# Delta rule's inverse: sums of two levels and the last sum move from identity matmuls to VectorE

## Chip, cores and metric

The kernel runs on one core of one Trainium2 chip. The metric is device time in microseconds (us). Before the change three runs gave 920.37, 923.16 and 924.47 us; the median is 923.16.

## The reference, cut to what matters

One layer of a generator: a modulated input, one input projection, two groups of heads on its columns, one output projection, a layer norm. The first group is a diagonal state-space scan (S5). The second is a gated delta rule with four heads and two directions, over 256 context and 1024 latent tokens in chunks of 64. For each chunk the reference solves a unit lower triangular system and then scans the chunks:

```python
a_mat = jnp.where(strict, bc[..., :, None] * kk * decay, 0.0)
sol = lax.linalg.triangular_solve(a_mat + eye, rhs, left_side=True, lower=True, unit_diagonal=True)
u0, w = sol[..., :Dv], sol[..., Dv:]
# then, for each chunk in turn:
u = ui0 - w_i @ s
o = g_i * (q_i @ s) + qk_i @ u
s = gl_i * s + k_i.T @ u
```

The kernel takes chunks of 128 tokens instead and forms the inverse of the triangular matrix itself. The change lies in that inverse.

## The kernel before, in words

Up to about 540 us the kernel computes the modulation, the projections, the S5 group and the convolutions of the second group. Then comes the delta rule, until about 845 us, and last the end of the last head's scan with the output projection and the norm.

In the delta rule each of the four heads has ten chunks of 128 tokens. One call of `tbatch` (line 1173) makes the inverses of two chunks in both directions, four 128x128 matrices u = 0 to 3 side by side in tiles of 128x512; five calls make a head, 20 the kernel. A call builds the decay (`mg`, `pd`, `dec`, lines 1185 to 1211), the products of keys and of keys with queries (`pk`, 1212), the matrix `tt` and its fp16 copy `t16`, and the start of the inverse in `xz`, an fp16 tile of 128 x 4 x 2 x 128 which holds the inverse's blocks (xs) and their transposes (zs).

The inverse then grows by doubling blocks, in the loop of line 1269 over levels l = 1 to 6. A level is four steps in a row: eight small matmuls into the bank `pp` (line 1274); a masked copy of them into the fp16 tile `pad` (VectorE at line 1282, at level 6 ScalarE at 1277); sixteen small matmuls into the bank `px` (line 1298); and `xz` plus `px` back into `xz`. This last step has two forms. At the levels in `ACTL`, which are 1 and 3, line 1290 first puts the old `xz` into the bank by a product with the identity, the sixteen matmuls add to it, and ScalarE copies the bank to `xz` (line 1309). At levels 2, 4 and 5 there is no identity product and VectorE adds bank and `xz` (line 1311). Level 6 is copied by ScalarE (line 1304).

After the loop one step of iteration refines the inverse: the residual `r16` (lines 1315 to 1325), the bank `pzz` = residual times zs (1328), a scaled copy `dl` (1330), residual times `dl` added to the same bank (1332), and then 1024 times zs added to it by two products with `i1k`, which is 1024 times the identity (line 1337; the tile is made at line 111). `finish` copies the bank to the fp32 tile `zf` with the factor 1/1024 on ScalarE (line 1360).

All banks of one call share one PSUM bank of its own (`bank`, tag t0 to t3): four calls can be under way, and within a call a bank must be emptied before the next step writes it. `scan_head` (line 1370) then runs ten steps for both directions: `s1` (matmul, line 1386), `rr` (VectorE, 1390), `s2` with `zf` (1395), `uu` (ScalarE, 1399), `s3` (1402), `st` (VectorE, 1409), and for latent chunks the output (1416, 1417). Between all this `fill` queues pieces of a part of the output projection (`poa`, `part_out`) behind given matmuls.

The engines run in parallel, each in a fixed order of its own. That order is worked out when the kernel is built, by the framework's planner from its own estimate of each instruction (the kernel is built with `schedule_with_timeline_sim=True`, line 1673): batches, the scan of the head before and the output projection are mixed by it. What is changed in one instruction can therefore change the order elsewhere.

Of the kernel before, what the change touches and what calls it, by code (L numbers as in the profile page):

```python
# [11 lines left out]
F16 = mybir.dt.float16  # L12
BF16 = mybir.dt.bfloat16
I32 = mybir.dt.int32
AF = mybir.ActivationFunctionType
ALU = mybir.AluOpType
# [3 lines left out]
P = 128  # L20
# [21 lines left out]
def tile_hybrid_block(  # L42
# [30 lines left out]
    V, S, G, T, Q = nc.vector, nc.scalar, nc.gpsimd, nc.tensor, nc.sync  # L73

    per = ctx.enter_context(tc.tile_pool(name="per", bufs=1))
# [13 lines left out]
    def bc(ap, shape):  # L89
        return ap.to_broadcast(shape)  # L90

    ident = per.tile([P, P], F32, name="ident")
# [3 lines left out]
        out=sel,  # L96
# [10 lines left out]
    V.tensor_copy(idbf, ident)  # L107
    nid2k = per.tile([P, P], F16, name="nid2k")
    V.tensor_scalar(nid2k, ident, -2048.0, None, op0=ALU.mult)
    i1k = per.tile([P, P], F16, name="i1k")  # L110
    V.tensor_scalar(i1k, ident, 1024.0, None, op0=ALU.mult)
    tri = per.tile([P, 2, P], F32, name="tri")
    trir = per.tile([P, 2, P], F32R, name="trir")
    negm = per.tile([P, 2, P], BF16, name="negm")
# [42 lines left out]
    for t, i, base, cm, step in ((tri, 0, 0, -1, 1), (tri, 1, 0, 1, -1), (trs, 1, -1, -1, 1), (trs, 0, -1, 1, -1)):  # L157
        G.affine_select(
            out=t[:, i, :], in_=t[:, i, :], pattern=[[step, P]], compare_op=ALU.is_ge, fill=0.0,
# [913 lines left out]
    for l in range(1, 7):  # L1073
# [4 lines left out]
        for d in range(2):  # L1078
            V.tensor_scalar(
                lvm[:, l - 1, d].rearrange("p c f -> p (c f)"), eq, half[:, d, l:l + 1], -1.0 / 2048,  # L1080
                op0=ALU.mult, op1=ALU.mult,
# [49 lines left out]
    for st in ORD.split():  # L1131
        name, _, hold = st.partition(">")
# [17 lines left out]
                glu_stage()  # L1150


    ACTL = (1, 3)
    L6, MASKP, NOID, XZP = True, True, True, True
    QTB = 2
    PTB, QGB, WB = 6, 5, 6
# [16 lines left out]
    def tbatch(hd, hs, cp, si):  # L1173
# [5 lines left out]
        def bank(n):  # L1179
            return psT.tile([P, 512], F32, tag=f"t{si}", name=n + nm, bufs=1)  # L1180

        def tl(shape, dt, tag, n):
            return gt_.tile(shape, dt, tag=tag, name=n + nm, bufs=TB[tag])
# [17 lines left out]
        for d in range(2):  # L1201
            for i in range(2):
                u = d * 2 + i
# [3 lines left out]
            if MASKP:  # L1207
                G.affine_select(
                    out=dec[:, d], in_=dec[:, d], pattern=[[0, 2], [1 - 2 * d, P]], compare_op=ALU.is_ge, fill=0.0,
# [3 lines left out]
        for i in range(2):  # L1213
            T.matmul(pk[:, i * P:(i + 1) * P], kT[:, c0 + i, :], kT[:, c0 + i, :], start=True, stop=True)
            if lat:
                T.matmul(
                    pk[:, (2 + i) * P:(3 + i) * P], kT[:, c0 + i, :], qT[:, (c0 + i) * P:(c0 + i + 1) * P],
                    start=True, stop=True,
# [13 lines left out]
        xz = tl([P, 4, 2, P], F16, "xz", "xz")  # L1232
# [4 lines left out]
        if XZP:  # L1237
            G.affine_select(
                out=xz[:, 3::-2], in_=mb.rearrange("p (d c) f -> p d c f", d=2), pattern=[[0, 2], [0, 2], [1, P]],
                compare_op=ALU.not_equal, fill=1.0, base=0, channel_multiplier=-1,  # L1240
            )
        else:
# [5 lines left out]
            out=thi, in_=t16, pattern=[[0, 4], [1, P]], compare_op=ALU.not_equal, fill=2048.0,  # L1248
# [5 lines left out]
            out=tlo, in_=tlo, pattern=[[0, 4], [1, P]], compare_op=ALU.not_equal, fill=0.0,  # L1254
# [6 lines left out]
        def scat(t, b, gs, n):  # L1261
            base = t
            return bass.AP(tensor=base.tensor, offset=base.offset, ap=[list(base.ap[0]), [gs + b, 2], [2 * b, n], [1, b]])
# [5 lines left out]
        for l in range(1, 7):  # L1269
# [16 lines left out]
            px = bank(f"px{l}_")  # L1286
            on_act = l in ACTL
            xo = scat(xz[:, 0, 0], b, 512, 256 // b)
# [30 lines left out]
        r16 = tl([P, 4, P], F16, "r16", "r16")  # L1319
        S.activation(r16.rearrange("p u f -> p (u f)"), prr, AF.Copy, scale=-0.5)  # L1320
        if NOID:
            G.affine_select(
                out=r16, in_=r16, pattern=[[0, 4], [1, P]], compare_op=ALU.not_equal, fill=0.0,
                base=0, channel_multiplier=-1,
            )
        pzz = bank("pzz")
        for u in range(4):
            T.matmul(pzz[:, u * P:(u + 1) * P], r16[:, u, :], zs[u], start=(u == 0), stop=(u == 3))
        dl = tl([P, 4, P], F16, "dl", "dl")
        S.activation(dl.rearrange("p u f -> p (u f)"), pzz, AF.Copy, scale=1.0 / 1024.0)  # L1330
        for u in range(4):
            T.matmul(
                pzz[:, u * P:(u + 1) * P], r16[:, u, :], dl[:, u, :], start=False, stop=False,
                skip_group_check=True,
            )
        for d in range(2):
            T.matmul(
                pzz[:, d * 256:(d + 1) * 256], i1k, xz[:, 3 - 2 * d].rearrange("p c f -> p (c f)"),
                start=False, stop=(d == 1), skip_group_check=True,
            )  # L1340
        def gqs():
            qg = gs.tile([P, 2, 2, P], F32, tag="qg", name="qg" + nm, bufs=QGB)
            for i in range(2):
                Q.dma_start(
                    qg[:, :, i, :], d_gr[c0 + i:c0 + i + 1, hd].to_broadcast([P, 2, P]),
                )
            qv = qT[:, c0 * P:(c0 + 2) * P].rearrange("p (o c f) -> p o c f", o=1, c=2)
            G.tensor_tensor(qg, qg, bc(qv, [P, 2, 2, P]), op=ALU.mult)
            hs["qg"][cp] = qg
# [5 lines left out]
        def finish():  # L1355
            if lat and cp not in hs["qg"]:
                gqs()
            kt = hs["kt"]
            zf = gs.tile([P, 2, 2, P], F32, tag="zf", name="zf" + nm, bufs=WB)
            S.activation(zf.rearrange("p d c f -> p (d c f)"), pzz, AF.Copy, scale=1.0 / 1024.0)  # L1360
            ks = gs.tile([P, 2, 2, P], F32, tag="ks", name="ks" + nm, bufs=WB)
            G.tensor_tensor(
                ks, bc(kt[:, None, c0:c0 + 2, :], [P, 2, 2, P]), bc(gx[:, :, 1, c0:c0 + 2, hd, None], [P, 2, 2, P]),
                op=ALU.mult,
            )
            hs["zf"][cp], hs["ks"][cp] = zf, ks
# [226 lines left out]
    for si in range(NPAD):  # L1593
        mkpads(si)
    fin = [tbatch(0, hs[0], CPS[n], n) for n in range(2)]
    wos.append(rp.tile([P, 2, 4, D], F32R, tag="wo", name="wo_a"))
    load_wo(0)
# [13 lines left out]
    for hd in range(HEADS):  # L1611
        if hd:
            hs[hd] = head_prep(hd)
            head_prep2(hd, hs[hd])
        for cp in CPS:
            if nb > 1:
                tbatch(hd, hs[hd], cp, nb % NS)()
            nb += 1
            if nb == 4 * NS:
                for _ in filler:  # L1620
                    pass
                wos.append(rp.tile([P, 2, 4, D], F32R, tag="wo", name="wo_b"))
                load_wo(1)
        if hd < HEADS - 1:
            scan_head(hd, hs[hd])
            head_out(hd, hs[hd])
# [51 lines left out]
```

## Time and profile before

| | |
|---|---|
| median of three runs | 923.16 us |
| profiled execution | 919.21 us, span 917.5 us |
| TensorE matmul busy | 814.1 us (89%) |
| VectorE busy | 672.5 us (73%) |
| ScalarE busy | 415.2 us (45%) |
| GpSimd busy | 392.1 us (43%) |

In the rows below PE is TensorE's matmuls, PEld its weight loads, DVE is VectorE, ACT is ScalarE, POOL is GpSimd; L1290 is line 1290. Matmuls overlap one another, so the durations of neighbours don't add up to the time that they take. The profiled execution is one run; its span is what the profile covers, and 1.7 us lie around it.

### The profile page before, as it was taken

The numbers are of one execution on the slowest core, as the hardware profiler recorded it, in microseconds if no ns is written. First come the engines' busy times: TensorE is split into PE (matmuls) and PEld (weight loads), VectorE is DVE, ScalarE is ACT, GpSimd is POOL, SyncE is SP. The second block draws the span as 40 slices with busy tenths as digits, with TensorE's granted clock in tenths as the row PEclk, the third lists the DMA queues.
The fourth block names the chain that finished last, engine by engine and source line by source line (L and its number), as shares of the span: only waits on it lengthen the run. The fifth ranks groups of instructions, "written<-read, shape, count | busy, mean of one in ns | idle before, by whom it ended". The sixth has DMA issues, their size and how long they took to land. (4 is left out here: it accounts for less than half of the span.)

```text
span 917.5 us, 17187 instructions
## 1 busy us (share of the span) xinstructions
PE 814.1 (89%) x6553; PEld 674.8 (74%) x6553; DVE 672.5 (73%) x1318; ACT 415.2 (45%) x944; POOL 392.1 (43%) x463
## 2 busy tenths in 40 slices
PE   4988999997898999996899896899989889789994
PEld 2656897785786788874688674687988778678882
DVE  7988986996776778799573388567685585676686
ACT  1321435324434444431544376465763473556353
POOL 3215240007897940100311078874874485441163
PEclk9999999999798999998799897799999999999998
DMA  9981557412304232243454476421135234315332
GB/s 245 302 158 42 196 157 232 146 36 79 132 24 142 106 104 84 94 159 93 122 148 134 148 269 213 145 75 59 48 109 161 82 115 156 128 41 182 126 126 93
DMA packets 120125, 119.49 MB, mean 130 GB/s; under 512 B 21406, under 2 KB 95702, under 8 KB 119914
## 3 DMA queue, kind: packets, MB, share of 16 engines
q1 hardware_dynamic: 101946, 85.42, 32.7%
q10 hardware_dynamic: 18096, 32.97, 9.5%
q8 instruction: 51, 0.84, 0.4%
q14 instruction: 32, 0.26, 0.1%
HBM read 81.33 MB, written 37.04 MB: 129 GB/s over the span
## 5 line engine op out<-in xcount | busy, mean ns | idle before, releaser
L713 POOL TENSOR_TENSOR rta<-ebuf,ar 128x64 f32<-128x64 f32 x38 | 24.8, 653 | 85.3 <-DVE ebuf L688 82.6
L847 POOL COPY hq<-ebuf 64x1024 f32<-64x1024 f32 x8 | 16.4, 2068 | 93.9 <-DVE ebuf L688 58.5
L1187 POOL TENSOR_TENSOR mg<-tri,ghi 128x512 fp32r<-128x512 f32 x20 | 23.2, 1162 | 70.7 <-PE pd L1195 35.4
L1282 DVE TENSOR_TENSOR pad<-pp,lvm 128x256 f16<-128x256 f32 x100 | 40.5, 416 | 16.3 <-PE pp L1274 15.6
L141 PE MATMUL pjz<-h_hi,wtz 128*128 128x512 f32 x128 | 52.0, 406 | 0.1
L142 PE MATMUL pjz<-h_lo,wtz 128*128 128x512 f32 x128 | 52.0, 407 | 0.0
L143 PE MATMUL pjz<-h_hi,wtz 128*128 128x512 f32 x128 | 51.3, 401 | 0.0
L1298 PEld LDWEIGHTS <-xz 128*128 128x128 f16 x480 | 37.6, 101 | 18.5 <-issue 12.5
L1298 PE MATMUL px<-pad,xz 128*128 128x64 f16 x480 | 42.8, 198 | 7.0 <-DVE pad L1282 6.5
L1311 DVE TENSOR_TENSOR xz<-px,xz 128x512 f16<-128x512 f32 x60 | 40.6, 684 | 10.8 <-PE px L1298 8.8
L759 DVE SCALAR_TENSOR_TENSOR cak<-crk,cwt,cak 128x945 f32<-128x945 f32 (+2 forms) x32 | 39.3, 1229 | 7.3 <-ACT cak L749 6.9
L759 DVE SCALAR_TENSOR_TENSOR caq<-crq,cwt,caq 128x945 f32<-128x945 f32 (+2 forms) x32 | 39.2, 1224 | 7.2 <-ACT caq L749 5.3
L1298 PE MATMUL px<-xz,pad 128*128 128x64 f16 x480 | 42.8, 198 | 0.0
L759 DVE SCALAR_TENSOR_TENSOR cav<-crv,cwt,cav 128x945 f32<-128x945 f32 (+2 forms) x32 | 39.4, 1231 | 4.1 <-ACT cav L749 3.8
L1274 PE MATMUL pp<-xz,t 128*128 128x64 f16 x480 | 33.1, 197 | 7.1 <-DVE xz L1311 3.3
L803 POOL TENSOR_TENSOR kss<-kss,mhalf 128x4 f32<-128x4 f32 (+1 forms) x12 | 15.6, 1309 | 55.5 <-DVE kss L802 55.5
L1399 ACT ACTIVATE uu<-s 128x128 f32<-128x128 f32 x80 | 21.0, 275 | 38.7 <-PE s L1395 38.5
L1390 DVE SCALAR_TENSOR_TENSOR rr<-s,ngx,vt 128x128 f32<-128x128 f32 x72 | 24.5, 344 | 17.0 <-PE s L1386 16.4
L1274 PEld LDWEIGHTS <-t 128*128 128x128 f16 x480 | 27.5, 101 | 12.4 <-issue 10.4
L141 PE MATMUL u<-wu,h_lo 128*128 128x512 f32 x64 | 29.3, 458 | 5.5 <-DVE h_lo L562 5.5
L822 ACT ACTIVATE csz<-pjz 128x512 f32<-128x512 f32 x16 | 9.2, 597 | 54.9 <-PE pjz L143 43.0
L1395 PE MATMUL s<-rr,zf 128*128 128x128 f32 x144 | 31.4, 303 | 2.3 <-DVE rr L1390 1.8
(514 smaller groups left out, 3029.1 us busy)
## 6 DMA issues: line engine op xcount, KB each, us to landing
wad<-in_w_ada_dram SPq DMA_DIRECT2D x16, 512.0 KB, 6.3
xk<-in_x_dram SPq DMA_DIRECT2D x8, 512.0 KB, 6.5
d_e<-et ACTq DMA_DIRECT2D x8, 512.0 KB, 2.8
etl<-d_e SPq DMA_DIRECT2D x8, 512.0 KB, 4.3
wg<-in_w_ada_dram SPq DMA_DIRECT2D x8, 512.0 KB, 5.7
wrz<-in_w_in_dram SPq DMA_DIRECT2D x8, 512.0 KB, 3.9
d_z<-csz ACTq DMA_DIRECT2D x8, 512.0 KB, 2.9
xr<-in_x_dram SPq DMA_DIRECT2D x8, 512.0 KB, 5.4
```

The source lines that it names most:

```text
L141: T.matmul(ps, ll, rh, start=first, stop=False)
L142: T.matmul(ps, lh, rl, start=False, stop=False)
L143: return T.matmul(ps, lh, rh, start=False, stop=last)
L713: G.tensor_tensor(ta, prev, ar, op=ALU.mult)
L759: clast[typ, hd] = V.scalar_tensor_tensor(out=o, in0=rv[:, y0 + dy:y1 + dy, x0 + dx:x1 + dx], scalar=cwt[:, t, (dy + 1) * 3 + dx + 1:(dy + ...
L1187: G.tensor_tensor(mg[:, i], bc(tri[:, 0:2, None, :], [P, 2, 2, P]), bc(gsrc[:, :, c0:c0 + 2, hd, None], [P, 2, 2, P]), op=ALU.mult,)
L1274: T.matmul(pp[:, u * 64:(u + 1) * 64], t16[:, u, :], cols(xs[u], b, u // 2), start=True, stop=True)
L1282: V.tensor_tensor(scat(pad[:, 0, :], b, 256, 128 // b), pp[:, :256].rearrange("p (d n b) -> p d n b", d=2, b=b), lvm[:, l - 1].rearrange(" ...
L1298: ins = T.matmul(o, lt, rt, start=not on_act, stop=not on_act or w == 3 and i == 1)
L1311: V.tensor_tensor(xo, pxv, xo, op=ALU.add)
L1390: V.scalar_tensor_tensor(out=rn, in0=p1_[:, :P], scalar=ngx[:, d, ch, hd:hd + 1], in1=rr, op0=ALU.mult, op1=ALU.add,)
L1395: ins = T.matmul(p2_[:, :P], hs["zf"][cp][:, d, i, :], rr, start=True, stop=True)
```

## The change

`ACTL` becomes empty, so that levels 1 and 3 are done as 2, 4 and 5 are: no identity product, and VectorE adds bank and `xz` (line 1311) where ScalarE copied (line 1309). The two products of line 1337 go, with the tile `i1k`; in their place `finish` makes `zf` on VectorE as bank/1024 plus the zs half of `xz`, where ScalarE copied the scaled bank.

```diff
-    i1k = per.tile([P, P], F16, name="i1k")
-    V.tensor_scalar(i1k, ident, 1024.0, None, op0=ALU.mult)
...
-    ACTL = (1, 3)
+    ACTL = ()
...
             T.matmul(
-                pzz[:, u * P:(u + 1) * P], r16[:, u, :], dl[:, u, :], start=False, stop=False,
+                pzz[:, u * P:(u + 1) * P], r16[:, u, :], dl[:, u, :], start=False, stop=(u == 3),
                 skip_group_check=True,
             )
-        for d in range(2):
-            T.matmul(
-                pzz[:, d * 256:(d + 1) * 256], i1k, xz[:, 3 - 2 * d].rearrange("p c f -> p (c f)"),
-                start=False, stop=(d == 1), skip_group_check=True,
-            )
...
-            S.activation(zf.rearrange("p d c f -> p (d c f)"), pzz, AF.Copy, scale=1.0 / 1024.0)
+            V.scalar_tensor_tensor(
+                out=zf, in0=pzz.rearrange("p (d c f) -> p d c f", d=2, c=2), scalar=1.0 / 1024.0, in1=xz[:, 3::-2],
+                op0=ALU.mult, op1=ALU.add,
+            )
```

## Rows read from the trace of the kernel before

**Rows 1.** The page's first table: busy us (share of the span), instructions.
```profile
PE 814.1 (89%) x6553; PEld 674.8 (74%) x6553; DVE 672.5 (73%) x1318; ACT 415.2 (45%) x944; POOL 392.1 (43%) x463
```

**Rows 2.** Busy time by stretch: start:end, length, busy us (instructions), clock, DMA, GB/s.
```profile
580.00:845.00 265.00, 242.46 (x2801) 213.36 (x2799) 176.30 (x414) 151.96 (x435) 152.29 (x184) 0.97 0.32 104
...
545.00:845.00 300.00, 266.05 (x2993) 232.22 (x2991) 206.66 (x455) 169.37 (x468) 184.16 (x214) 0.94 0.36 116
```

**Rows 3.** The same view, 605 to 625 and 685 to 705: their sum.
```profile
sum 40.00, PE 39.90 PEld 35.81 DVE 23.47 ACT 21.69 POOL 26.11; mean PE 19.95 PEld 17.90 DVE 11.74 ACT 10.85 POOL 13.06
```

**Rows 4.** The same view, four other stretches: the first, and the sum of all.
```profile
567.00:577.00 10.00, 4.95 (x58) 3.81 (x59) 9.99 (x16) 4.00 (x8) 10.00 (x11) 0.67 0.91 297
...
sum 40.00, PE 28.20 PEld 23.84 DVE 39.23 ACT 20.27 POOL 30.82; mean PE 7.05 PEld 5.96 DVE 9.81 ACT 5.07 POOL 7.71
```

**Rows 5.** Groups, 545 to 845: busy us, mean ns of one, idle before, releasers.
```profile
L1311 DVE TENSOR_TENSOR xz<-px,xz 128x512 f16<-128x512 f32 x60 | 40.6, 684 | 10.8 <-PE px L1298 8.8 <-ACT pad L1277 1.0 <-ACT uu L1399 0.8
...
L1309 ACT ACTIVATE xz<-px 128x512 f16<-128x512 f32 x40 | 23.6, 593 | 14.0 <-PE px L1298 8.8 <-DVE ml L877 3.5 <-DVE rr L1390 1.2
...
L1290 PE MATMUL px<-xz,id 128*128 128x512 f16 x40 | 16.3, 408 | 1.5 <-DVE pad L1282 1.4
...
L1360 ACT ACTIVATE zf<-pzz 128x512 f32<-128x512 f32 x20 | 11.9, 594 | 8.2 <-PE pzz L1337 8.2
...
L1525 DVE SCALAR_TENSOR_TENSOR y<-xr,poa 128x512 f32<-128x512 f32 x16 | 11.0, 688 | 26.4 <-PE poa L143 17.9 <-DMA xr<-in_x_dram 7.4 <-PE px L1298 1.0
...
L1337 PE MATMUL pzz<-xz,i1k 128*128 128x256 f16 x40 | 7.9, 280 | 0.0
```

**Rows 6.** TensorE's instructions in order of time: start us, us, what.
```profile
592.32 0.38 PE L1290 MATMUL px<-xz,id 128*128 128x512 f16 x1
592.53 0.22 PE L1298 MATMUL px<-pad,xz 128*128 128x64 f16 x2
...
592.99 0.38 PE L1337 MATMUL pzz<-xz,i1k 128*128 128x256 f16 x2
593.21 0.22 PE L1298 MATMUL px<-pad,xz 128*128 128x64 f16 x2
```

**Rows 7.** Busy time by stretch, with the granted clock behind POOL's.
```profile
575.00:585.00 10.00, 7.63 (x94) 6.29 (x94) 6.14 (x12) 4.06 (x9) 10.00 (x11) 0.53 0.85 272
```

**Rows 8.** Chain of waits: shares of 580 to 845, then pieces (start us, us).
```profile
by line: PE px L1298 6.7%; DMA xr<-in_x_dram 6.3%; PE poa L141 5.4%; DMA qg<-d_gr 5.2%; issue 5.2%; PE poa L143 4.7%; PE poa L142 4.7%; PE s L1395 4.3%; PE s L1386 3.7%; PE s L1402 3.5%; PE pp L1274 3.1%; PE s L1416 2.7%; PE pd L1195 2.5%; 
...
582.08 0.43 PE px L1290
...
821.87 0.23 PE px L1290
...
822.55 0.22 PE pzz L1337 x2
...
825.77 0.60 ACT zf L1360
```

**Rows 9.** VectorE's instructions in order of time.
```profile
567.62 0.68 DVE L1224 SCALAR_TENSOR_TENSOR tt<-pkk,dec 128x512 f32<-128x512 f32 x1
568.21 0.68 DVE L1230 TENSOR_TENSOR pt<-pkk,dec 128x512 f32<-128x512 f32 x1
```

**Rows 10.** Busy time by stretch of line 1309 alone, then of line 1360 alone.
```profile
567.00:577.00 10.00, 1.18 (x3) 0.67 0.91 297
...
751.00:757.00 6.00, 1.20 (x2) 1.00 0.06 22
```

**Rows 11.** TensorE's waits, 545 to 845: us in total, times, longest us.
```profile
PE px L1298 <- DVE pad L1282: 6.5, 9, 1.8
...
PE pp L1274 <- DVE xz L1311: 3.3, 6, 0.8
...
PE pp L1274 <- ACT xz L1309: 1.9, 2, 1.1
```

## The prediction, made before the changed kernel was seen

> **What bounds the kernel now.** I read the page's first table, then the busy time by stage, the groups of instructions of the stage that the change touches, TensorE's waits, the chain of waits, and last the single instructions around a few of the removed matmuls. By the page TensorE is the busiest engine (89% of the span), VectorE second (73%) [rows 1]. The changed instructions, one of the start apart, lie between 545 and 845 us. The main part of that stage, 580 to 845, has TensorE busy for 242.5 of 265 us, VectorE 176.3, ScalarE 152.0, GpSimd 152.3 [rows 2]. So TensorE is the first bound there, with gaps of some 22 us. The bound is not the same all along: in two stretches of 20 us TensorE is busy for 39.9 of 40 us [rows 3], but in four others, 567 to 577, 669 to 676, 751 to 757 and 795 to 812, VectorE is, for 39.2 of 40 us [rows 4]. The change takes from TensorE and gives to VectorE, so both kinds of stretch count.
>
> **What goes: TensorE.** Line 1290 (the identity product that opens the bank of levels 1 and 3) runs 40 times, line 1337 (the last sum) 40 times in 20 pairs. The table gives 408 and 280 ns for one [rows 5], but matmuls overlap, so the price is the step from one start to the next: line 1290 starts at 592.32 and the next matmul at 592.53, which is 0.21 us; a pair of line 1337 starts at 592.99 and the next matmul at 593.21, 0.22 us [rows 6]. That is at TensorE's full clock. About five of the 40 start before 585, where the granted clock is 0.53 of full in ten us, thus mostly at the lower of its two levels [rows 7]; they cost twice as much. TensorE issues 40 x 0.21 + 5 x 0.21 + 20 x 0.22 = 13.9 us less. That is the upper bound. The lower bound is nothing: where TensorE would wait anyway, the time was free. Between them the chain of waits decides. Line 1290 stands on it with 20 pieces of 0.21 to 0.43 us, 5.4 us in all, and line 1337 with 15 pairs, nearly all 0.22 us, 3.4 us in all (a long and a typical piece stand) [rows 8]. I take 5.4 + 3.4 = 8.8 us; the other 20 and 5 are off the chain. The identity product cannot hide in the wait for the masked pad: all levels of a batch use one bank, and that is free for line 1290 only when line 1282 on VectorE has read it, the very instruction that the other matmuls of the level wait for. Line 111, a small VectorE operation of the start, I count as nothing: it runs half a millisecond before the stage.
>
> **What goes: ScalarE.** 40 copies of line 1309 at 593 ns and 20 of line 1360 at 594 ns, 35.5 us of its 169.4 between 545 and 845 [rows 2, 5]. ScalarE is not the bound, so this frees nothing by itself. Seven of the copies are on the chain, 3.8 us in all, such as 0.60 us of zf at 825.77 [rows 8].
>
> **What comes: VectorE.** 40 sums more of line 1311's kind, which is there 60 times at 684 ns, and 20 scaled sums for zf. The zf form (bank and fp16 in, fp32 out, 128x512) is not in the trace; nearest are line 1525, the same operation with an fp32 operand at 688 ns, and line 1311 with an fp16 one at 684 [rows 5]. I take 686; the ends are 594 (if it cost what ScalarE's copy costs) and 780 (as far above), which over 20 is 1.9 us either way. On the path a sum is thus 0.09 us longer than the copy: 7 x 0.09 = +0.6 us. In a full queue the step counts: line 1224 starts at 567.62 and the next at 568.21, so 0.60 us for one of this shape [rows 9]. VectorE's load rises by 60 x 0.60 = 36 us, from 206.7 to 243 of 300 [rows 2].
>
> Where VectorE is full this is paid in full. Of the moved copies eight of line 1309 (3, 1, 2, 2) and three of line 1360 (2 and 1) lie in the four full stretches (the first row of each line stands) [rows 10]: 11 x 0.60 = 6.6 us. Three of them are in 567 to 577, where GpSimd too is busy for 10.00 of 10 us [rows 4] and holds the next batches back, so I take the other eight: +4.8 us (bounds 0 and 6.6). The other 49 go where VectorE has gaps. They delay what is queued behind them: pad masks (line 1282), and rr and st of the scan (lines 1390 and 1409), for which TensorE waits. The waits come along too: ScalarE stood 8.8 us for px before line 1309 and 8.2 us for pzz before line 1360 [rows 5]; VectorE will now stand there, with the same rr, st and pads behind it. TensorE's five longest waits on VectorE add to 6.5 + 3.3 + 3.0 + 1.8 + 1.4 = 16.0 us (the first two stand) [rows 11]. If VectorE's gaps, 93 us of 300, shrink to 57 and these waits grow as the inverse, that is 16.0 x (93/57 - 1) = +10.1 us; if the planner, which sets each engine's order, keeps the urgent operations in front, nothing. No row is nearer to one end: half, +5.0 us.
>
> The four xz buffers are held until zf is made, not until line 1337 a step before; the buffer's next writer belongs to the fourth batch after, so nothing. No DMA is moved.
>
> **The sum.** -8.8 + 0.6 + 4.8 + 5.0 = +1.6 us. The profiled execution took 919.21 us (span 917.5 and 1.7 around it) and would take 920.8; it lies 4.0 us under the median of the runs, 923.16. On the median the sum is 924.8, so I say 925: no change that a measurement of this kernel can tell (0.5%, which is 4.6 us).
>
> Against the change speaks a rule of the Trainium skill ("Perfetto Trace Analysis", Identifying the Most-Contended Engine): TensorE's headroom is to be judged by its weight-load time, because matmuls overlap, the other engines by occupancy, and the most contended engine is the one to relieve. By weight loads TensorE is at 213.4 of 265 us in the stage [rows 2], and 176 + 36 us would bring VectorE level with it: by that rule the slower rival below is the outcome. The stretches where TensorE is solid while VectorE is at 23.5 of 40 us [rows 3] speak against it, those of rows 4 for it.
>
> **Rivals.**
> - VectorE becomes the bound (slower). Its queue is served in order, and each of the 60 sums delays one thing that TensorE needs by half its length: 60 x 0.30 = 18 us, in place of the 5.0; with 6.6, 0.6 and -8.8 this is +16.4, some 939 us. For it: the full stretches, and that pads and sums of VectorE are already what TensorE waits for longest [rows 11]. Against it: 93 us of gaps. It decides from where more than a quarter of the added time reaches TensorE (8.8 of 36 us).
> - TensorE's time comes back whole (faster). -13.9 + 0.6 + 2 (a few sums in the full stretches) = -11.3, some 912 us. For it: TensorE waited 3.3 us in all for the 60 sums on VectorE and 1.9 us for the 40 copies on ScalarE [rows 11], 55 and 48 ns for each, so the exchange itself costs nearly nothing. Against it: a third of the removed matmuls are off the chain.
> - The removed matmuls don't arrive as a gain, nor the sums as a loss. The planner writes a new order from its own costs, and the chain holds 6.3% of loads of xr and 5.2% of loads of qg in the stage [rows 8], 16.7 and 13.8 us that no engine's work shortens. Then -3 to +6, which lies in the forecast's own range.
>
> **Chances.** The near balance (920 to 933, the planner's case in it) 0.42, of which 0.24 within 0.5% of 923.2 and 0.18 above; VectorE as bound 0.23, all slower; TensorE's time back 0.35, of which 0.31 faster by over 0.5% and 0.04 within. Faster 0.31, same 0.28, slower 0.41. The range goes from 907 (the 912, with 5 us that a new order can add) to 943 (the 939 and 4).
>
> **What would show it.** In the changed profile lines 1290 and 1337 are gone, TensorE's busy time in the stage falls by up to 14 us, VectorE's rises by 36 to 41, ScalarE's falls by 35. Right: TensorE's waits for VectorE grow by 5 to 10 us and the stage keeps its length. Wrong to the fast side: those waits stay at 16 us and the stage is 10 us shorter. Wrong to the slow side: VectorE has far more of the chain, with rr and st late behind sums of 684 ns. Wrong altogether: the time moved outside the stage.

## The result, and the profile after

The changed kernel takes 926.55 us (median of 11 runs), the kernel before 921.7 us on the same chip: a ratio of 1.0069, 95% interval 1.0047 to 1.0091, or +6.4 us (4.3 to 8.4). So it is slower, by little more than the 0.5% that the prediction called measurable. The profiled execution took 926.32 us, its span 924.5. One run of f2_change_held below (1296.98 us at a granted clock of 0.557, beside 0.93 to 0.94 in its other five) is in no ratio.

The page's first table (busy us, share of the span, instructions):

```profile
PE 809.0 (88%) x6473; PEld 673.1 (73%) x6473; DVE 705.9 (76%) x1377; ACT 386.8 (42%) x884; POOL 388.2 (42%) x463
```

Against [rows 1] VectorE has 33.4 us more, ScalarE 28.4 less, TensorE 5.1 less. By stretch (start:end, length, then busy us and instructions of TensorE, its weight loads, VectorE, ScalarE, GpSimd, the granted clock, DMA share, GB/s):

```profile
580.00:845.00 265.00, 236.49 (x2706) 209.78 (x2705) 206.50 (x468) 122.82 (x371) 149.28 (x184) 0.95 0.32 102
...
545.00:845.00 300.00, 257.06 (x2862) 227.09 (x2861) 239.13 (x509) 137.64 (x400) 180.25 (x213) 0.91 0.36 113
```

[Rows 2] show the same stretches of before: TensorE 9.0 us less over the 300 us, VectorE 32.5 more. The groups of the moved sums, 545 to 860 (busy us, mean ns of one, idle before, releasers), stand at the price expected from [rows 5]; the zf form, which no row of before showed, takes 685 ns, and 686 was taken:

```profile
L1309 DVE TENSOR_TENSOR xz<-px,xz 128x512 f16<-128x512 f32 x100 | 67.1, 683 | 5.8 <-PE px L1296 4.6 <-ACT uu L1395 0.7 <-PE pp L1272 0.2
...
L1353 DVE SCALAR_TENSOR_TENSOR zf<-pzz,xz 128x512 f32<-128x512 f32 x20 | 13.7, 685 | 2.4 <-PE pzz L1330 2.4
```

Lines 1272, 1280, 1296 and 1309 of the changed kernel are 1274, 1282, 1298 and 1311 of before. TensorE's waits, 545 to 870 (us in total, times, longest us):

```profile
PE pp L1272 <- DVE xz L1309: 10.8, 14, 3.6
PE px L1296 <- DVE pad L1280: 7.2, 10, 2.0
PE pkk L1212 <- DMA kT<-d_qkv: 3.7, 2, 3.0
```

The first was 3.3 us [rows 11], the second 6.5. All rows of this view in which TensorE waits for VectorE add to 16.9 us in the kernel before and 25.2 in this one. The third, a wait for the load of kT, was 0.2 us in before.

So far this reads as VectorE's load reaching TensorE. Where the time is lost says something else. The instruction that makes zf marks the end of each of the 20 batches; the rows give durations min/median/max and the first and last start, for before and then for the changed kernel:

```profile
L1360 ACT ACTIVATE zf<-pzz x20: 577/597/614, 593.5 to 842.5; 128x512 f32<-128x512 f32 x20
```

```profile
L1353 DVE SCALAR_TENSOR_TENSOR zf<-pzz,xz x20: 676/683/692, 593.7 to 853.4; 128x512 f32<-128x512 f32 x20
```

The first batch ends at the same time (593.5 and 593.7), the last 10.9 us later; what follows it is 3.9 us shorter (917.5 - 842.5 = 75.0, 924.5 - 853.4 = 71.1). Inside, the two kernels are level until the 12th batch (733.5 and 731.5); from the 12th to the 13th before takes 20.1 us, the changed kernel 31.3. There, in a stretch of 30 us in which the scan of the third head begins, it falls 9 us behind. What follows is not level: the lag is 12.7 us at the 16th batch, 4.0 at the 17th and 10.9 at the 20th, since the planner has mixed the batches with the other work in another order. A count that doesn't hang on the batches is the number of matmuls shared by both kernels that TensorE has started: the changed kernel reaches the count of before at 740 us 1.4 us earlier, that of 750 us 6.9 us later, and after swings between 5 and 10 us that of 870 us 8.1 us later. So most of the loss comes in this stretch; the later swings were not followed up. The stretch, in before and then in the changed kernel:

```profile
733.00:763.00 30.00, 27.55 (x337) 24.05 (x336) 23.19 (x58) 18.59 (x60) 21.53 (x28) 1.00 0.38 129
```

```profile
733.00:763.00 30.00, 22.93 (x228) 19.41 (x228) 20.19 (x48) 13.17 (x44) 17.71 (x22) 0.89 0.35 118
```

Over the 30 us every engine does less here, VectorE too, so it is not a greater load on VectorE that makes the stretch longer. What differs is SP's queue: its two loads of 640 KB for the next head, with two loads of qg (128 KB each) between them (start us, us of issue), before and then changed:

```profile
734.37 0.33 SPq L1162 DMA_DIRECT2D kT<-d_qkv  x1
734.79 0.90 SPq L1344 DMA_DIRECT2D qg<-d_gr  x2
735.78 1.05 SPq L1169 DMA_DIRECT2D kt<-d_kt  x1
```

```profile
734.14 0.33 SPq L1167 DMA_DIRECT2D kt<-d_kt  x1
734.56 0.90 SPq L1337 DMA_DIRECT2D qg<-d_gr  x2
735.51 0.46 SPq L1160 DMA_DIRECT2D kT<-d_qkv  x1
```

kt and kT have changed places, so kT is now the fourth load of the group and was the first. On the chain of waits kT is a piece of 4.67 us in before, and here of 7.88:

```profile
734.37 4.67 DMA kT<-d_qkv
```

```profile
735.51 7.88 DMA kT<-d_qkv
```

3.0 us of it are TensorE's wait for kT, the longest of its rows above. What follows it, from 743 on, by stretch, and last the middle one of the three in before:

```profile
743.00:748.00 5.00, 4.57 (x39) 4.43 (x40) 2.47 (x7) 1.99 (x4) 3.09 (x4) 0.66 0.18 56
748.00:753.00 5.00, 3.39 (x39) 2.47 (x38) 5.00 (x10) 0.56 (x2) 5.00 (x7) 1.00 0.00 0
753.00:758.00 5.00, 4.21 (x44) 3.67 (x43) 4.43 (x12) 1.90 (x5) 0.20 (x1) 0.66 0.01 3
```

```profile
748.00:753.00 5.00, 4.95 (x80) 4.40 (x81) 4.48 (x14) 3.63 (x10) 3.90 (x5) 1.00 0.01 2
```

After the wait the granted clock is 0.66 for 5 us, so part of them ran at the lower of the two levels (1.2 against 2.4 GHz); then VectorE and GpSimd are full and TensorE is busy for only 3.4 of 5 us, and the clock is 0.66 again. In before it is 1.00 in all three, with TensorE busy for 4.95 us of the middle one. So for 5 us the two other engines are what is full here, behind the wait for kT (TensorE waits 1.4 us of it for line 1434 of VectorE, the row scalings of a head's output). The loads are no instruction that the change touches; their order came from the planner.

### The profile page after: what moved, and what is told of

It reads as the page before. It is cut to its first block, busy times and chain, and to the rows that moved or that the text cites. A ratio compares the mean times of both kernels' runs of the same rounds, so it can differ in the third digit from the quotient of the medians.

```text
span 924.5 us, 17089 instructions
## 1 busy us (share of the span) xinstructions
PE 809.0 (88%) x6473; PEld 673.1 (73%) x6473; DVE 705.9 (76%) x1377; ACT 386.8 (42%) x884; POOL 388.2 (42%) x463
## 5 line engine op out<-in xcount | busy, mean ns | idle before, releaser
L1309 DVE TENSOR_TENSOR xz<-px,xz 128x512 f16<-128x512 f32 x100 | 67.1, 683 | 5.8 <-PE px L1296 4.6
L845 POOL COPY hq<-ebuf 64x1024 f32<-64x1024 f32 x8 | 16.4, 2074 | 93.8 <-DVE ebuf L686 58.5
L801 POOL TENSOR_TENSOR kss<-kss,mhalf 128x4 f32<-128x4 f32 (+1 forms) x12 | 15.6, 1309 | 56.1 <-DVE kss L800 56.1
L1320 POOL TENSOR_SCALAR_AFFINE_SELECT r<-r 128x512 f16<-128x512 f16 x20 | 12.9, 646 | 54.9 <-ACT r L1318 54.9
L1398 PE MATMUL s<-uu,ks 128*128 128x128 f32 x144 | 32.8, 314 | 1.2 <-ACT uu L1395 1.2
```

The costliest lines, as they stand in the source:

```text
L1309: V.tensor_tensor(xo, pxv, xo, op=ALU.add)
L1398: ins = T.matmul(p3_[:, :P], hs["ks"][cp][:, d, i, :], uu, start=True, stop=True)
```

## The experiments

Two theories stood at the start. **Load**: what was moved decides; TensorE's 13.9 us buy something, VectorE's 60 sums cost more. **Order**: the planner, which writes each engine's order anew from its own costs, decides, and the work itself nearly cancels. Of the 6473 matmuls that the traces of both kernels have, at least 1130 stand in another order after the change.

**Four parts in the planner's own order.** All ratios are to the kernel before on the same chip, five rounds, with the 95% interval behind them; us are the ratio's share of before's median. First the sums of levels 1 and 3 alone, the last sum as before:

```diff
-    ACTL = (1, 3)
+    ACTL = ()
```

> Only the first part of the change: levels 1 and 3 are summed by VectorE without the identity product; the last sum stays with the two products of line 1337 and ScalarE's copy. The whole change cost 6.4 us (ratio 1.0069 of 921.7). Theory A (parts add: TensorE's removed time comes back with what stood on the chain, and VectorE's longer queue costs more than that): the chain gives 5.4 us for line 1290, and two thirds of VectorE's cost, which must be 8.8 + 6.4 = 15 us in all, so +10 - 5.4 = +4.6 us, a ratio near 1.005. Theory B (the planner's new order makes the difference, the load does not): no such share; anything from 0.993 to 1.010, and not the sum of parts with the kernel that has the other half.

Measured 0.9959 (0.9937 to 0.9982), 918.31 us: 3.8 us faster, although it gives VectorE 40 of the 60 sums (698.8 us busy over the span, 672.5 in before [rows 1]). Then the last sum alone:

```diff
-            S.activation(zf.rearrange("p d c f -> p (d c f)"), pzz, AF.Copy, scale=1.0 / 1024.0)
+            V.scalar_tensor_tensor(out=zf, in0=pzz..., scalar=1.0 / 1024.0, in1=xz[:, 3::-2], op0=ALU.mult, op1=ALU.add)
```

> Only the second part: zf is summed by VectorE, line 1337 and its tile are gone; levels 1 and 3 stay with the identity product and ScalarE. Theory A: -3.4 us of the chain for line 1337 and a third of VectorE's 15 us, +5, so +1.6 us, a ratio near 1.002; with the kernel that has only the levels it adds to the whole change (1.007). Theory B: anything from 0.993 to 1.010, and the two parts don't add to 1.007.

Measured 1.0033 (1.0004 to 1.0062). The two parts add to -0.08%, the whole is +0.69%: no account in which each part has a price of its own can give that. Third, TensorE's gain without VectorE's cost:

```diff
-            if on_act:
-                T.matmul(px, id16, xo, start=True, stop=False)
...
-        for d in range(2):
-            T.matmul(pzz[:, d * 256:(d + 1) * 256], i1k, ...)
```

> TensorE's side alone: the products of lines 1290 and 1337 are left out and nothing comes to VectorE; ScalarE copies the banks as before, so the old xz is missing from levels 1 and 3 and from zf (those sums are left out). Theory A: what the removed matmuls are worth, -8.8 us by the chain (bounds 0 and -13.9), a ratio near 0.990. Theory B: the removed time is worth nothing of its own; between 0.995 and 1.005.

Measured 1.0018 (0.9994 to 1.0042): 13.9 us less of issue (the prediction's estimate) on the busiest engine, and nothing gained. Fourth, VectorE's cost without TensorE's gain, by 60 useless sums:

```diff
+    TB = dict(..., scr=1)
...
+                V.tensor_tensor(tl([P, 2, 2, P], F16, "scr", f"scr{l}"), xz[:, 0:4:2], bc(tri...), op=ALU.add)
```

> VectorE's side alone: the kernel before with 60 more VectorE sums of 128x512 into a scratch tile that nobody reads, 40 behind ScalarE's copies of levels 1 and 3 and 20 behind its copy to zf; all matmuls stay (three constant tiles that nothing uses are dropped to make room). Theory A: VectorE's longer queue costs 15 us by the measured sum, 10 by the forecast: a ratio from 1.010 to 1.017, with TensorE's waits on VectorE 5 to 10 us longer. Theory B: VectorE has 93 us of gaps between 545 and 845 and nobody waits for these sums, so 0 to 2 us, within 0.998 to 1.003.

Measured 1.1903 (1.1862 to 1.1944), which is a fault of the experiment: one scratch buffer served all batches, so that a batch's first useless sum had to come behind the last one of the batch before, in the planner's order too. From first to last zf its 20 batches take 419.9 us instead of 249.0. Waits of GpSimd and of VectorE in it, over the span:

```profile
POOL r L1318 <- ACT r L1316: 163.6, 16, 20.9
```

```profile
DVE scrz L1357 <- ACT zf L1356: 72.5, 16, 8.7
```

It says nothing of VectorE's load.

**The order held.** Since each of these kernels was planned anew, the next four hold it. The kernel builds the other variant first, reads the order of each engine (SP's queue included) off it, and ties every two neighbours among the instructions that both variants have by a dependency that only orders them and adds no wait:

```diff
+        for p, q in zip(order, order[1:]):
+            tc.add_manual_dep(own_[q], own_[p].name, dep, reason="held order")
```

Only the changed instructions themselves are still placed by the planner. The traces bear it out: of the 6473 shared matmuls, GpSimd's 463 operations and SP's 283 DMA issues not one of f1_nomatmul_held, f2_change_held and f4_load_held stands elsewhere than in before, and not one of f3_before_in_new_order elsewhere than in the changed kernel. One control was not run, before's work tied to its own order; that the ties cost nothing is taken, not measured. First the matmuls left out in before's order:

> Lines 1290 and 1337 are left out as in the run before (the sums that they carried are missing), but now every engine's other instructions are held in the order that the planner gave the kernel before. Theory A (the removed matmuls were worth what stood on the chain, and the new order of the free run hid it): -8.8 us, a ratio near 0.990. Theory C (TensorE's removed time only becomes waiting, in any order): 0.998 to 1.002, as in the free run (1.0018).

Measured 0.9958 (0.9929 to 0.9988): -3.9 us (-6.5 to -1.1), where planned freely it was +1.7. So TensorE's relief is worth something, about a quarter of its 13.9 us (between 1.1 and 6.5 us). Then the whole change in before's order:

> The whole change, with all instructions that both kernels share held in the planner's order of the kernel before, engine by engine; only the new VectorE sums are placed by the planner between them. Theory A (load: VectorE's queue costs more than TensorE's time gives): 1.007, as in the free run. Theory B (the 6 us came with the planner's new order, a quarter of TensorE's instructions stand elsewhere): near 1.000, between 0.994 and 1.003.

Measured 1.0089 (1.0056 to 1.0122): +8.2 us. And the work of before in the changed kernel's order:

> The work of the kernel before (identity products, ScalarE's copies), with the shared instructions held in the order that the planner gave the changed kernel; only lines 1290, 1309, 1337 and 1360 are placed freely between them. Theory A (load): 1.000 or a little more, since VectorE is relieved again and TensorE has its 13.9 us back. Theory B (order): the new order costs the 6 us by itself, 1.005 to 1.012.

Measured 1.0092 (1.0062 to 1.0121): +8.5 us with no instruction of the change in it. Last the load, 60 useless sums in before's order, with scratch that ties no batches:

> The kernel before in its own held order, with 60 more VectorE sums of 128x512 (40 behind ScalarE's copies of levels 1 and 3, 20 behind its copy to zf) into scratch that holds no other batch back: the earlier load run wrote a single scratch buffer and so tied each batch to the one before. Three constant tiles that nothing uses are dropped for room. Theory A: the queue costs 10 to 15 us, 1.011 to 1.016. Theory B: the 93 us of VectorE's gaps take most of the 36 us, 1.000 to 1.005.

Measured 1.0252 (1.022 to 1.0284): +23.2 us. Its sums were dearer than meant (groups, 545 to 870):

```profile
L1328 DVE TENSOR_TENSOR cond<-xz,tri 128x512 f16<-128x512 f16 x20 | 19.9, 993 | 6.3 <-ACT xz L1326 6.3
...
L1328 DVE TENSOR_TENSOR scr<-xz,tri 128x512 f16<-128x512 f16 x20 | 17.6, 881 | 2.1 <-ACT xz L1326 2.1
...
L1392 DVE TENSOR_TENSOR t<-zf,tri 128x512 f16<-128x512 f32 x20 | 15.8, 792 | 1.3 <-ACT zf L1390 1.1
```

That is 19.9 + 17.6 + 15.8 = 53.3 us of load, where the prediction's step of 0.60 us would make 36, and 0.44 us of time for each us. A useless sum reads only SBUF, while a moved sum reads a bank and SBUF, and the trace tells the two apart. Of the 60 useless sums 26 took over 700 ns, up to 1758, and each of these ran beside a GpSimd operation for at least a third of its time; the 27 with GpSimd beside them for under a fifth of theirs took 675 to 694. In the changed kernel 57 of line 1309's 100 sums ran beside GpSimd for over four fifths of their time and took 683 on average, 693 at most. GpSimd too is busy for 8.2 us more over the span (400.3 against 392.1 [rows 1]). So load on VectorE does cost, also where it has gaps, but the 0.44 belongs to sums of this kind and may be too much for the moved ones.

The work and the order, crossed, in us against before:

| | before's order | the changed kernel's order |
|---|---|---|
| before's work | 0 | +8.5 |
| the changed work | +8.2 | +6.4 |

Each alone costs 8 us, both together 6.4, not 16.7. The traces show which is at work in the kernel as built. In f3_before_in_new_order zf, SP's loads and TensorE's wait for kT read:

```profile
L1389 ACT ACTIVATE zf<-pzz x20: 579/598/617, 595.4 to 855.2; 128x512 f32<-128x512 f32 x20
```

```profile
736.05 0.33 SPq L1179 DMA_DIRECT2D kt<-d_kt  x1
736.48 1.20 SPq L1366 DMA_DIRECT2D qg<-d_gr  x2
737.73 0.46 SPq L1172 DMA_DIRECT2D kT<-d_qkv  x1
```

```profile
PE pkk L1224 <- DMA kT<-d_qkv: 4.0, 2, 3.1
```

```profile
733.00:763.00 30.00, 23.69 (x242) 20.63 (x240) 18.61 (x45) 14.22 (x46) 19.49 (x24) 0.89 0.32 108
```

From first to last zf it takes 259.8 us, the changed kernel 259.7, before 249.0; from the last zf to the end of its span of 926.3 us 71.1, the changed kernel 71.1, before 75.0; from the 12th to the 13th batch 30.1, against 31.3 and 20.1. It has the swapped loads, again with two of qg between them, the wait for kT and the emptier stretch with its clock of 0.89. By the count of shared matmuls it loses 7.6 us between 740 and 750 us of before (the changed kernel 8.3), and it has the later swings too. The changed kernel's profile has the shape of its order, in these figures to within 1.2 us, with the old work as with the new. In f2_change_held, new work in the old order, the same places read otherwise: kT is issued first, TensorE waits 0.3 us for it, the 12th to the 13th batch take 22.5 us. There the loss shows in TensorE's waits on VectorE (545 to 870):

```profile
PE pp L1284 <- DVE xz L1323: 10.0, 8, 3.6
PE px L1310 <- DVE pad L1292: 7.2, 13, 1.8
PE pp L1284 <- DVE xz L1332: 5.8, 10, 1.1
```

All TensorE's waits on VectorE in it add to 35.3 us, against 16.9 of before, 19.9 of f1_nomatmul_held, 22.0 of f3_before_in_new_order and 25.2 of the changed kernel. So by these waits the old order is bad for the new work, in which VectorE comes late (18.4 us more of them); the new order, made for it, has 10.1 us less of them and the longer stretch at the third head instead.

One part of f2_change_held's +8.2 us stays open. Where VectorE multiplies graw by zts, ahead of the stage and of every changed instruction, it is already late in its profile; before, and then this kernel:

```profile
L936 DVE TENSOR_TENSOR graw<-graw,zts x3: 1210/1212/1217, 532.4 to 539.1; 128x1024 f32<-128x1024 f32 x3
```

```profile
L946 DVE TENSOR_TENSOR graw<-graw,zts x3: 1211/1211/1218, 536.6 to 543.3; 128x1024 f32<-128x1024 f32 x3
```

These 4.2 us lie in the first 140 us (the last of TensorE's matmuls into u starts at 139.4 against 135.2), where TensorE waits 9.6 us for h_lo of VectorE instead of 5.5. The changed kernel and f3_before_in_new_order start this multiplication at 532.3, f1_nomatmul_held at 532.4; of the thirteen profiles without e4_load six are 3 to 8 us late, among them that of the fastest kernel, e1_levels, by 6.4. It looks like scatter between executions: in three of the six (e1_levels, g1_levels_held, g3_levels_on) the profiled execution is the slowest of all runs of its kernel. But f2_change_held's is no slower than its others (931.25 us; they go from 926.75 to 931.27), so for it the record doesn't tell. If only the profiled execution started late, the +8.2 us stand; if all of them did, some 4 us are not the stage's.

**The parts in before's order.** If the parts have prices once the order is held, they should add now:

> Only levels 1 and 3 go to VectorE, and all shared instructions are held in the planner's order of the kernel before. In its own order this gave 0.9959, and the whole change in the held order 1.0089. Theory A (load, in a held order the parts add): two thirds of the VectorE side (12 us by the held runs: 8.2 + 3.9) less 5.4/8.8 of TensorE's 3.9, so +5.6 us, 1.006. Theory B (what the levels alone gained came from a lucky order only): the same, 1.004 to 1.008; if the levels truly cost nothing on VectorE, 0.994 to 0.998 here too.

Measured 1.0118 (1.0072 to 1.0163): +10.9 us (its profile is 6.8 us late ahead of the stage).

> Only the last sum goes to VectorE, all shared instructions held in the planner's order of the kernel before. Theory A (load; parts add to the 1.0089 of the whole): a third of VectorE's 12 us less 1.5 us, +2.6 us, 1.003. Theory D (the last sum is the dear one, since VectorE stands in front of it until TensorE has finished pzz): most of the 8.2 us, 1.006 to 1.009.

Measured 1.0058 (1.0031 to 1.0086): +5.3 us. They add to 1.76% and the whole is 0.89%; the intervals (some 0.5% either way on the sum, 0.3% on the whole) leave this open, so adding is not shown here either. What is shown is the size of the order, as far as the ties cost nothing: the same 40 sums, with the same matmuls gone, cost +10.9 us in before's order and gain 3.8 in the one planned for them. That is 15 us from the order, on a change of 6.

**A better version.** The levels alone beat both kernels. If VectorE's load is what is left, moving the 32 row scalings of line 1438 to ScalarE should gain more:

```diff
-        V.tensor_scalar(on, hs["acc"][:, i, :], hs["oss"][:, i:i + 1], None, op0=ALU.mult)
+        S.activation(on, hs["acc"][:, i, :], AF.Copy, scale=hs["oss"][:, i:i + 1])
```

> Levels 1 and 3 on VectorE as in the run before at 0.9959, and the 32 row scalings of line 1438 (128x128, 277 ns on VectorE, eight of them in the stretch of 751 to 757 us where VectorE is full) go to ScalarE, whose copies of levels 1 and 3 are gone. Planner's own order. Theory A (VectorE's load is what costs): 32 x 0.25 us = 8 us less load, at the third to half that the load runs showed a gain of 3 to 4 us, so about 0.992. Theory B (order): anything from 0.990 to 1.005.

Measured 0.9971 (0.9948 to 0.9995), beside the levels alone no gain. And the same in the kernel before:

> The kernel before with the 32 row scalings of line 1438 on ScalarE and nothing else changed, planner's own order. Theory A: VectorE has gaps there and ScalarE has its copies still, a gain of 0 to 3 us, 0.997 to 1.000. Theory B (order): 0.993 to 1.007 with no regard to the load.

Measured 1.0016 (0.9986 to 1.0046): nothing. VectorE's busy time over the span is 687.2 us in g3_levels_on against 698.8 in e1_levels, so the load fell there and the time didn't. In g4_before_on it is 671.4 against 672.5 [rows 1], 32 instructions fewer and hardly less load, so that run tells little. Both were planned anew. The fastest kernel stays e1_levels, 918.31 us.

## Why the prediction was right in its range and wrong in its side

- **The number.** 925 us was forecast and 926.55 measured, inside 907 to 943. Of the nearness 1.5 us are luck: the forecast counts from 923.16, the median of three runs, and before's eleven have 921.7. And the forecast's words were "no change that a measurement of this kernel can tell", +1.6 us, and it is +6.4. Slower had the largest of the three chances, 0.41; the likeliest single case was still the wrong side of the line.
- **The signs.** TensorE's waits on VectorE were to grow by 5 to 10 us and the stage to keep its length. They grew by 8.3, and the stage became 10.7 us longer. The second sign failed, and the sums are not needed for that: the stretch that grew is the same in f3_before_in_new_order, which has none of the moved ones.
- **The step that failed: the order.** The prediction had it as a rival, "-3 to +6, which lies in the forecast's own range", and gave the sum no term for it. The order alone costs +8.5 us with before's work. The range was drawn from loads on the chain (xr and qg [rows 8]); the load that came out late was kT, which the chain of before has too, and whose place on SP's queue the planner was free to change. "No DMA is moved" was true of the diff and false of the program.
- **TensorE's -8.8 us.** With the order held it is -3.9 (-6.5 to -1.1). The pieces of lines 1290 and 1337 on the chain were real, but when they go, other waits take over more than half: leaving them out raises TensorE's waits on VectorE from 16.9 to 19.9 us. Taken off the chain whole, they were overvalued. (Off the chain are 25 of 60, the single matmuls of line 1290 and the pairs of line 1337 counted, and not the third that a rival names.)
- **VectorE's +10.4 us** (0.6 + 4.8 + 5.0). In the held order the sums cost 8.2 + 3.9 = +12.1 us (some 4 either way), or about 8 if all runs of f2_change_held started late. By the useless sums' 0.44 us per us, 33.4 us of load would be 14.5, which may be too much (above). The runs agree with this term within their width; its split between full stretches and waits is untested.
- **The rivals.** VectorE as the bound, +16.4 us: not reached; e1_levels has 26 us more of VectorE than before and is the fastest. TensorE's time back whole, -11.3: not reached in either order. The third, the planner's order, is what came, above its bound of +6 when taken alone. The rule of the Trainium skill that spoke for the first ("Perfetto Trace Analysis", Identifying the Most-Contended Engine: optimize the most contended engine first) gets no fair test: in e3_nomatmul TensorE is busy for 10.0 us less than in before, in g3_levels_on VectorE for 11.6 less than in e1_levels, and neither gained anything that can be told, but both were planned anew. In the held order the relief of TensorE, the busiest by matmul time, gave 3.9 us (f1_nomatmul_held).

So by the sum's own terms, with the order held, +8.2 us instead of +1.6, most of it because TensorE's term came to less than half (4.9 us of the 6.6); and as built, +6.4 us in a profile that has the form of the new order. Why the orders planned for the single parts differ so (12.8 us from the 12th to the 13th batch with the levels alone, 26.7 with the last sum alone) is not settled. Nor is a long way from the 12th to the 13th a loss by itself: with the last sum alone first to last zf take 248.4 us, less than before's 249.0. The swap of kt and kT alone doesn't bring the wait: e1_levels has it as well,

```profile
735.77 0.33 SPq L1169 DMA_DIRECT2D kt<-d_kt  x1
736.55 0.33 SPq L1162 DMA_DIRECT2D kT<-d_qkv  x1
736.98 0.93 SPq L1344 DMA_DIRECT2D qg<-d_gr  x2
```

but there kT is the second load and the two of qg come behind it. It lands 4.84 us after its issue, and no wait for kT stands in its rows. What the wait for kT alone is worth was not tried.

## What to carry to other kernels

Where a planner writes the order of each engine from its own costs, an edit changes two things, the work and the order, and the second moved this kernel by -15 to +8.5 us on equal work, against the old order: give it a term and a range of its own. Time each part alone as well as the whole, since the best version here was one part of the change; and to learn what work is worth, hold the order of the rest. When a new profile is longer, first find the stretch that grew, by a mark that recurs in every batch and, since a planner can move the mark, by the work that the busiest engine has done by then, and compare what stands in the queues there, the loads' too, before blaming the engine whose load rose.

## What the runs showed of the hardware

- VectorE's sums of one shape (128x512) took 674 to 693 ns each where one operand came from a bank (lines 1309 and 1353 of the changed kernel), also beside GpSimd. Where all operands lay in SBUF they took 675 to 694 ns with GpSimd beside them for under a fifth of their time, and 26 of 60 took 737 to 1758 ns, all of them beside GpSimd (f4_load_held). Six that ran beside it for more than half of their time took 675 to 694 too, so the share of time alone doesn't decide.
- Where a load stands in a group on one queue shows in its landing. At the third head a load of 640 KB landed 3.9 to 4.7 us after its issue when it was the first of its group (kt 3.95 in the changed kernel and 3.86 in e1_levels, kT 4.67 in before and 4.02 in e2_last) and after 4.8 us as the second (kT 4.84 in e1_levels, kt 4.83 in e2_last). As the fourth, behind another of 640 KB and two of 128, kT was waited for until 7.88 us after its issue in the changed kernel and 7.66 in f3_before_in_new_order.
